# One PSUM bank for transposes, three for filter values, four buffers for decayed values in a filter stage

## The chip, the cores and the metric

The kernel runs on one core of a Trainium2 chip. TensorE (PE) multiplies matrices, VectorE (DVE), ScalarE (ACT) and GpSimd (POOL) work on tiles, SyncE (SP) issues most transfers. The metric is the device time of one execution in microseconds, the median of several runs.

## The reference

One layer of an encoder: a normalised input is projected, goes through a state-space branch (S5) and a Hyena branch, is merged, projected and normalised again. The change touches the implicit filters of the Hyena branch alone:

```python
h = jnp.sin(fr * (feats @ w1 + b1))
h = jnp.sin(fr * (h @ w2 + b2))
h = h @ w3                                           # (L, 4 * W): 2 orders, 2 directions
h = h * (jnp.exp(-t * jnp.abs(decay)) + HY_SHIFT)
h_fwd, h_bwd = h[:, :, 0], h[:, :, 1]
k = jnp.concatenate([h_fwd, jnp.zeros_like(h_fwd[:1]), jnp.flip(h_bwd[1:], axis=0)], axis=0)
k = k * lax.rsqrt(jnp.sum(k * k, axis=0, keepdims=True) + HY_EPS)
return jnp.fft.rfft(k, axis=0)
```

with L = 1024 positions and W = 1024 channels.

## The kernel before

The program is written in Python; a scheduler puts each engine's instructions into a fixed order, by the dependences, by its own model of durations and by the buffers that a pool has. An engine runs its instructions in that order and waits at each until its inputs are there and its buffer is free.

The filter stage comes first. It makes the filters in eight units of 256 channels in both directions (two orders, four quarters of the channels). Each unit has three parts.

`filter_time` goes over eight tiles of 128 positions, in the order 4, 5, 6, 7, 0, 1, 2, 3. For each, PE makes the filters' values g in one PSUM bank with two matmuls (L333, L334); ACT makes the exponential e (L336); DVE makes of both the decayed value, in the place of e (L338). ACT squares it into sq, for the first tile into acc (L342); POOL adds sq to acc (L357). The sum and the difference of the two directions (L349, L350) are made by POOL, for the first and the fourth tile (and in the first unit for the first six) by DVE. For the first four tiles they lie in so, which has one buffer, and are split in a rounded part sh (ACT, L109) and a rest sl (DVE, L113); for the last four they stay whole as ss and sd. For the fifth tile a memset of one row (L340) comes behind L338. At the end POOL folds acc (L362).

`filter_norm` sums acc over positions on PE into q (L371), which lies in the pool f_px, takes the inverse root on DVE in a chain of some twenty instructions on one or two elements per partition (L375, L119, L121, L125, L126, L381), turns a row with two transposes (L383) into the same bank and corrects ss (L386).

`filter_freq` makes the spectrum: PE multiplies sh and sl with cosines and sines (po, 96 matmuls of a unit, L404) and ss, sd (pe, 16 of two passes each, L414); ACT copies one pe to eo (L421), DVE makes ke (L425, L426) and ko (L429, L430) of it, SP stores ko. po and pe have two banks each. This part of a unit runs beside `filter_time` of the next.

Beside it `norm_in` normalises the input: its row norms go through the same chain (48 of DVE's small instructions), and then sixteen groups of four transposes (xt, L475, also in f_px) are read by ACT (xh, L479) and DVE (xl, L480). They must all be done before the projection begins (pps, L556), whose banks take the place of f_px and f_pg.

Of the kernel before, what the change touches and what calls it, by code (L numbers as in the profile page):

```python
# [9 lines left out]
F = mybir.dt.float32  # L10
# [4 lines left out]
PSUM = bass.MemoryType.PSUM  # L15
# [4 lines left out]
NCH = 256  # L20
# [80 lines left out]
class Trunk:  # L101
# [141 lines left out]
    def filters(self, ctx, top):  # L243
        tc = self.tc
        c2 = ExitStack()
        mk = lambda c, n, b, **kw: c.enter_context(tc.tile_pool(reuse_waits="tile", name=n, bufs=b, **kw))
        self.f_dve0, self.f_dve = (0, 1, 2, 3, 4, 5), (0, 3)
        sd = [None, mk(ctx, "f_sd1", 1)]
        self.f_w = mk(ctx, "f_work", 2)
        sd[0] = mk(c2, "f_sd0", 1, side="right")  # L250
        self.f_t = mk(c2, "f_time", 2, side="right")
        self.f_pk = mk(ctx, "f_pk", 1, space=PSUM)
        self.f_px, self.f_pg = (mk(c2, n, 2, space=PSUM, side="right") for n in ("f_px", "f_pg"))
        units = [(o, cq) for o in range(2) for cq in range(4)]
        sds = {}
        x = self.norm_in()
        for u in range(len(units) + 1):
            t = iter(())
            if u < len(units):
                t = self.filter_time(*units[u], sds, sd[u % 2])  # L260
            if u == 0:
                f = self.filter_freq(*units[0], sds)
                with tc.issue_after(self.f_sin.ins):
                    for i, _ in enumerate(t):
                        if i == 2:
                            self.f_next()
                        if i == 5:
                            with tc.issue_after(self.f_g.ins):
                                self.f_turn()
                        if i > 3:  # L270
                            next(f)
                f0 = 4
                continue
            if u > 1:
                f, f0 = self.filter_freq(*units[u - 1], sds), 0
            if u == len(units):
                self.filter_norm(*units[u - 1], sds)
                c2.close()
                self.weight_pools(top)
                self.proj_pools(top)  # L280
                self.prefetch()
            for i in range(12):
                next(t, None)
                if i == 0 and u < len(units):
                    with tc.high_priority(offset=40):
                        self.filter_norm(*units[u - 1], sds)
                if i >= f0:
                    with tc.issue_after(self.f_g.ins):
                        next(f)
                if i % 3 == 0:  # L290
                    with tc.issue_after(self.f_sq.ins):
                        next(x, None)
                if i == 6 and u + 1 < len(units):
                    self.filter_load(*units[u + 1])()
            for _ in t:
                pass
            next(f, None)
        for _ in x:
            pass
# [23 lines left out]
    def filter_time(self, o, cq, sds, pool):  # L323
        nc, I = self.nc, self.I
        wp = self.f_t
        fe, fo, ha, negt = self.fc
        w3h, w3l, decf = self.f_loaded.pop(0)
        sd_t = [None] * 8
        sds[o, cq] = [sd_t, None]
        for n, tt in enumerate((4, 5, 6, 7, 0, 1, 2, 3)):  # L330
            ps = self.f_pg.tile([128, 2 * NCH], F, name="g")
            tsl = slice(tt * 128, tt * 128 + 128)
            nc.tensor.matmul(out=ps, lhsT=ha[:, tsl], rhs=w3h, start=True, stop=False)  # L333
            self.f_g = nc.tensor.matmul(out=ps, lhsT=ha[:, tsl], rhs=w3l, start=False, stop=True)  # L334
            e = wp.tile([128, 2 * NCH], F, name="e", bufs=3)
            nc.scalar.activation(out=e, in_=decf, func=AF.Exp, scale=negt[:, tt:tt + 1])  # L336
            h = e
            nc.vector.scalar_tensor_tensor(out=h, in0=e, scalar=0.05, in1=ps, op0=ALU.add, op1=ALU.mult)  # L338
            if tt == 0:
                nc.vector.memset(h[0:1, NCH:2 * NCH], 0.0)  # L340
            sq = wp.tile([128, 2 * NCH], F, name="sq" if n else "acc", bufs=2 if n else 1)
            self.f_sq = nc.scalar.activation(out=sq, in_=h, func=AF.Square)  # L342
            if tt > 3:
                so = wp.tile([128, 2, NCH], F, name="so", bufs=1)
                sd = [so[:, 0], so[:, 1]]
            else:
                sd = [pool.tile([128, NCH], F, name=f"{m}{tt}") for m in ("ss", "sd")]
            eng = nc.vector if n in (self.f_dve0 if o == cq == 0 else self.f_dve) else nc.gpsimd
            eng.tensor_tensor(out=sd[0], in0=h[:, 0:NCH], in1=h[:, NCH:], op=ALU.add)  # L349
            eng.tensor_tensor(out=sd[1], in0=h[:, 0:NCH], in1=h[:, NCH:], op=ALU.subtract)  # L350
            if tt > 3:
                hl = [pool.tile([128, 2, NCH], R, name=f"{m}{tt}") for m in ("sh", "sl")]
                self.split(so, *hl, hi_eng="dve" if o == cq == 0 and n < 4 else "act")
                sd = hl
            sd_t[tt] = sd
            if n:
                nc.gpsimd.tensor_tensor(out=acc, in0=acc, in1=sq, op=ALU.add)  # L357
            else:
                acc = sq
            sds[o, cq][1] = acc  # L360
            if n == 7:
                nc.gpsimd.tensor_tensor(out=acc[:, 0:NCH], in0=acc[:, 0:NCH], in1=acc[:, NCH:], op=ALU.add)  # L362
            yield
# [1176 lines left out]
```

## Time and profile before

| | us |
|---|---|
| median of three runs | 1416.13 (1413.56 to 1418.54) |
| profiled execution | 1413.96 |
| its span | 1412.2 |

| engine | busy us | share of the span |
|---|---|---|
| PE | 1346.7 | 95% |
| PE's weight loads | 1135.9 | 80% |
| DVE | 1014.1 | 72% |
| ACT | 515.1 | 36% |
| POOL | 416.6 | 29% |

Busy is the time in which an engine has an instruction in work, including what that instruction waits for inside; idle time before an instruction is put down to what released it. Shares of the whole span are averages over stages with different limits.

### The profile page before, as it was taken

To read this page: it belongs to the slowest core of one execution; us is meant where nothing else is said; L and a number is where in the kernel's file an instruction comes from. 1 tells how busy PE (TensorE), PEld (TensorE's weight loads), DVE (VectorE), ACT (ScalarE), POOL (GpSimd) and SP (SyncE) were. 2 spreads that over 40 slices of the span, in tenths; PEclk is the share of its full clock that TensorE was granted. 3 is DMA by queue.
4 is the path that set the end of the run, shared out by engine and by line. 5 is a ranking of instruction groups with operands and counts; after the bars stand their busy time and mean duration, and the time that the engine had idled before them with its cause. 6 is when DMAs were issued, how large, how long until landed. Compare 5 with 4: busy or idle time off the path is not lost.

```text
span 1412.2 us, 19536 instructions
## 1 busy us (share of the span) xinstructions
PE 1346.7 (95%) x7219; PEld 1135.9 (80%) x7219; DVE 1014.1 (72%) x1934; ACT 515.1 (36%) x737; POOL 416.6 (29%) x343
## 2 busy tenths in 40 slices
PE   5888899999999999999999997999999999999997
PEld 3777798888888887788788885998888889878886
DVE  7999997699599887414479997663899836843632
ACT  5576664222332333333322222443222234422422
POOL 3766675000000000223112213743013223322322
PEclk9999999999999999999999998999999999999999
DMA  8222224865695554566985588769888988755431
GB/s 278 94 78 75 77 100 146 200 173 137 164 301 132 124 124 103 134 173 155 307 244 173 172 241 264 216 179 315 258 268 268 292 247 245 220 161 134 139 112 64
DMA packets 188556, 257.24 MB, mean 182 GB/s; under 512 B 23069, under 2 KB 144153, under 8 KB 185724
## 3 DMA queue, kind: packets, MB, share of 16 engines
q1 hardware_dynamic: 148492, 151.32, 34.0%
q0 software_dynamic: 12608, 43.79, 15.6%
q10 hardware_dynamic: 27360, 60.88, 12.0%
q8 instruction: 57, 0.93, 0.3%
q14 instruction: 39, 0.32, 0.1%
HBM read 147.49 MB, written 76.82 MB: 159 GB/s over the span
## 4 chain that ended last, share of the span: by engine, by line
PE 72%; DVE 18%; DMA 5%; issue 3%; ACT 1%; POOL 1%; SPq 0%; ACTq 0%; DVEq 0%; POOLq 0%
PE pps L556 43%; PE ops L1441 6%; PE iv L643 5%; PE po L404 4%; PE fwo L695 3%; DMA zc<-c_zc_lo_d 2%; PE pe L414 2%; PE pps L536 2%; DVE rsq_h L125 2%; DVE e L338 1%; PE fwe L695 1%; DMA d_y<-x 1%; DVE st L1274 1%; PE zt L680 1%; DVE st L1272 1%
## 5 line engine op out<-in xcount | busy, mean ns | idle before, releaser
L512 POOL DMA_DIRECT2D wlo<-wraw x76 | 66.3, 872 | 673.3 <-ACT wlo L511 530.2
L556 PE MATMUL pps<-xh,whi 128*128 128x512 f32 x848 | 214.2, 400 | 3.2 <-DVE cv L581 3.2
L556 PE MATMUL pps<-xl,whi 128*128 128x512 f32 x848 | 212.3, 397 | 0.0
L556 PE MATMUL pps<-xh,wlo 128*128 128x512 f32 x848 | 210.2, 396 | 0.0
L556 PEld LDWEIGHTS pps<-xh,whi 128*128 128x128 f32 x848 | 158.0, 189 | 39.5 <-ACT wlo L511 3.6
L556 PEld LDWEIGHTS pps<-xh,wlo 128*128 128x128 f32 x848 | 157.9, 188 | 36.8
L556 PEld LDWEIGHTS pps<-xl,whi 128*128 128x128 f32 x848 | 157.3, 188 | 36.3 <-issue 0.2
L510 ACT CAST whi<-wraw 128x1024 fp32r<-128x1024 f32 (+1 forms) x76 | 74.7, 982 | 285.7 <-PE pps L556 254.9
L404 PE MATMUL po<-sh,fo 128*128 128x256 f32 x512 | 101.1, 292 | 6.0 <-DVE sh L111 5.1
L643 PE MATMUL iv<-ic,y 128*128 128x256 f32 (+1 forms) x752 | 97.2, 287 | 5.5 <-POOL y L113 3.1
L643 PEld LDWEIGHTS iv<-ic,y 128*128 128x128 f32 x752 | 95.4, 194 | 8.1 <-POOL y L113 4.0
L404 PEld LDWEIGHTS po<-sh,fo 128*128 128x128 f32 x512 | 84.0, 197 | 8.3 <-DVE sh L111 6.1
L357 POOL TENSOR_TENSOR acc<-acc,sq 128x512 f32<-128x512 f32 x56 | 75.9, 1356 | 24.5 <-ACT sq L342 23.0
L511 ACT ACTIVATE wlo<-whi 128x1024 fp32r<-128x1024 f32 (+1 forms) x76 | 74.9, 985 | 20.7 <-PE pps L556 20.6
L113 DVE TENSOR_TENSOR y<-yraw,y 128x512 fp32r<-128x512 f32 x60 | 55.0, 938 | 28.2 <-ACT y L109 28.2
L404 PE MATMUL po<-sl,fo 128*128 128x256 f32 x256 | 74.2, 290 | 1.0 <-DVE sl L113 1.0
L579 DVE SCALAR_TENSOR_TENSOR cv<-pps,cw,cv 128x1023 f32<-128x1023 f32 x24 | 30.7, 1281 | 59.5 <-ACT cv L578 59.5
L109 ACT CAST y<-yraw 128x512 fp32r<-128x512 f32 x64 | 39.0, 619 | 55.9 <-DMA yraw<-d_y 27.4
L404 PEld LDWEIGHTS po<-sl,fo 128*128 128x128 f32 x256 | 50.4, 197 | 2.2 <-DVE sl L113 1.3
L578 ACT ACTIVATE cv<-pps,cb,cw 128x1024 f32<-128x1024 f32 x24 | 29.0, 1208 | 62.1 <-PE pps L556 43.9
L333 PE MATMUL g<-w3h,ha 128*128 128x512 f32 x64 | 33.3, 520 | 18.6 <-DVE e L338 17.6
L695 PE MATMUL fwo<-z,zc 128*128 128x256 f32 x384 | 49.9, 283 | 0.0
(447 smaller groups left out, 2788.7 us busy)
## 6 DMA issues: line engine op xcount, KB each, us to landing
wlo<-wraw POOLq DMA_DIRECT2D x64, 512.0 KB, 5.7
wraw<-w_in SPq DMA_DIRECT2D x56, 512.0 KB, 5.2
kspec<-ko SPq DMA_DIRECT2D x32, 512.0 KB, 3.6
kt<-kspec SPq DMA_DIRECT2D x32, 512.0 KB, 5.1
yraw<-d_y SPq DMA_DIRECT2D x64, 256.0 KB, 5.3
d_y<-x ACTq DMA_DIRECT2D x28, 512.0 KB, 5.5
d_m<-cv ACTq DMA_DIRECT2D x16, 512.0 KB, 2.6
d_z<-z ACTq DMA_DIRECT2D x8, 1024.0 KB, 5.5
```

The source lines that it names most:

```text
L109: nc.scalar.copy(out=hi, in_=src)
L113: e.tensor_tensor(out=lo, in0=src, in1=hi, op=ALU.subtract)
L333: nc.tensor.matmul(out=ps, lhsT=ha[:, tsl], rhs=w3h, start=True, stop=False)
L357: nc.gpsimd.tensor_tensor(out=acc, in0=acc, in1=sq, op=ALU.add)
L404: nc.tensor.matmul(out=po[:, part], lhsT=fo[a][:, 12 * (jj % 2) + b], rhs=sd[4 + i][d][:, part], start=n == 0 and part == 0, stop=n == 11 ...
L510: nc.scalar.copy(out=hi, in_=raw)
L511: nc.scalar.activation(out=lo, in_=hi, func=AF.Copy, scale=-1.0)
L512: nc.gpsimd.dma_start(out=lo, in_=raw, accum_op=ALU.add)
L556: self.summed = nc.tensor.matmul(out=ps[:, hf * 512:hf * 512 + 512], lhsT=w[:, kc], rhs=part(x, kc, hf), start=a == 0 and p == 0 and kc == ...
L643: self.rotated = nc.tensor.matmul(out=dst, lhsT=lhsT, rhs=self.ic[b, j][:, cols], start=first, stop=last)
L695: nc.tensor.matmul(out=out, lhsT=zc[a][:, b], rhs=z[:, :, d, zi], start=start and n == 0, stop=stop and n == 3 * len(prods) - 1)
L1441: nc.tensor.matmul(out=pss[cs.start][:, 0:cs.stop - cs.start], lhsT=m[:, kc, ts], rhs=w[kc][:, cs], start=kc == 0 and p == 0, stop=kc == 7 ...
```

## The change

The pool f_px, which holds the groups of transposes and the norms' sums q, gets one PSUM bank in place of two; f_pg, which holds g, gets three in place of two. The tile e gets four buffers in place of three.

```diff
-        self.f_px, self.f_pg = (mk(c2, n, 2, space=PSUM, side="right") for n in ("f_px", "f_pg"))
+        self.f_px, self.f_pg = (mk(c2, n, b, space=PSUM, side="right") for n, b in (("f_px", 1), ("f_pg", 3)))
...
-            e = wp.tile([128, 2 * NCH], F, name="e", bufs=3)
+            e = wp.tile([128, 2 * NCH], F, name="e", bufs=4)
```

The scheduler writes another order of the filter stage for it. DVE, in the last unit, before: from the first sl of the unit to the second.

```order
L113 TENSOR_TENSOR sl_2317<-so,sh_2316 128x512
L429 TENSOR_TENSOR ko<-ke,po 128x512
L430 TENSOR_TENSOR ko<-ke,po 128x512
L338 SCALAR_TENSOR_TENSOR e<-e,g 128x512
L375 TENSOR_SCALAR qs<-q 128x2
L119 TENSOR_SCALAR nrm<-qs 128x2
L480 SCALAR_TENSOR_TENSOR xl<-xt,par,xh 128x512
L121 TENSOR_SCALAR qs<-qs 128x2
L338 SCALAR_TENSOR_TENSOR e<-e,g 128x512
L125 SCALAR_TENSOR_TENSOR rsq_h<-nrm,qs 128x1 x2
L113 TENSOR_TENSOR sl_2378<-so,sh_2377 128x512
```

The same engine and place after, from the first sl to the third.

```order
L113 TENSOR_TENSOR sl_2317<-so,sh_2316 128x512
L429 TENSOR_TENSOR ko<-ke,po 128x512
L430 TENSOR_TENSOR ko<-ke,po 128x512
L113 TENSOR_TENSOR sl_2378<-so,sh_2377 128x512
L338 SCALAR_TENSOR_TENSOR e<-e,g 128x512
L340 MEMSET e 1x256
L480 SCALAR_TENSOR_TENSOR xl<-xt,par,xh 128x512
L113 TENSOR_TENSOR sl_2406<-so,sh_2405 128x512
```

The three sl stand close together, and the norm's chain comes behind them. POOL in the last unit, before:

```order
L362 TENSOR_TENSOR acc<-acc 128x256
L349 TENSOR_TENSOR so<-e 128x256
L350 TENSOR_TENSOR so<-e 128x256
L357 TENSOR_TENSOR acc<-acc,sq 128x512 x2
L349 TENSOR_TENSOR so<-e 128x256
L350 TENSOR_TENSOR so<-e 128x256
L357 TENSOR_TENSOR acc<-acc,sq 128x512
L349 TENSOR_TENSOR ss_2467<-e 128x256
L350 TENSOR_TENSOR sd_2468<-e 128x256
L357 TENSOR_TENSOR acc<-acc,sq 128x512
```

and POOL there after:

```order
L362 TENSOR_TENSOR acc<-acc 128x256
L349 TENSOR_TENSOR so<-e 128x256
L350 TENSOR_TENSOR so<-e 128x256
L349 TENSOR_TENSOR so<-e 128x256
L350 TENSOR_TENSOR so<-e 128x256
L349 TENSOR_TENSOR ss_2467<-e 128x256
L350 TENSOR_TENSOR sd_2468<-e 128x256
L349 TENSOR_TENSOR ss_2487<-e 128x256
L350 TENSOR_TENSOR sd_2488<-e 128x256
L357 TENSOR_TENSOR acc<-acc,sq 128x512 x2
```

The two pairs of so stand side by side, and the accumulations have moved behind ss. PE behind the last g of the stage (the last L333, L334 of before), before:

```order
L475 MATMUL xt<-ident,xr 128x128 x4
L333 MATMUL g<-w3h,ha 128x512
L334 MATMUL g<-w3l,ha 128x512
L414 MATMUL pe<-sd_2193,fe 128x256
L414 MATMUL pe<-sd_2236,fe 128x256
L414 MATMUL pe<-ss_2192,fe 128x256
L414 MATMUL pe<-ss_2235,fe 128x256
L414 MATMUL pe<-sd_2144,fe 128x256
L414 MATMUL pe<-sd_2164,fe 128x256
L414 MATMUL pe<-ss_2143,fe 128x256
L414 MATMUL pe<-ss_2163,fe 128x256
```

and PE there after:

```order
L333 MATMUL g<-w3h,ha 128x512
L334 MATMUL g<-w3l,ha 128x512
L414 MATMUL pe<-sd_2193,fe 128x256
L414 MATMUL pe<-sd_2236,fe 128x256
L414 MATMUL pe<-ss_2192,fe 128x256
L414 MATMUL pe<-ss_2235,fe 128x256
L383 MATMUL q<-ident,qs 128x128 x2
L475 MATMUL xt<-ident,xr 128x128 x4
L414 MATMUL pe<-ss_2143,fe 128x256
L414 MATMUL pe<-ss_2163,fe 128x256
L475 MATMUL xt<-ident,xr 128x128 x4
L414 MATMUL pe<-sd_2144,fe 128x256
```

A norm's transposes and, with two more further down, four groups of xt have moved behind the last g.

## Rows read from the trace of the kernel before

**Rows 1.** Two windows: PE, PEld, DVE, ACT, POOL busy (instructions), PE clock, DMA.

```profile
20.00:228.00 208.00, 181.60 (x1070) 157.99 (x1068) 201.80 (x421) 133.05 (x241) 144.20 (x145) 0.95 0.29 105
...
228.00:290.00 62.00, 61.83 (x347) 53.68 (x348) 41.67 (x241) 15.58 (x19) 10.14 (x12) 1.00 0.81 207
```

**Rows 2.** Who waited for whom from 12 to 240 us: in total, times, longest.

```profile
PEld g L333 <- DVE e L338: 23.5, 15, 4.4
...
POOL ss L349 <- DVE e L340: 6.2, 2, 3.9
```

**Rows 3.** The same of DVE alone, from 20 to 228 us.

```profile
DVE sl L113 <- ACT sh L109: 2.8, 4, 1.0
DVE e L338 <- PE g L334: 0.9, 3, 0.4
```

**Rows 4.** DVE's groups, 20 to 228 us: count | busy us, mean ns | idle before.

```profile
L113 DVE TENSOR_TENSOR sl<-so,sh 128x512 fp32r<-128x512 f32 x32 | 25.3, 790 | 2.9 <-ACT sh L109 2.8
L125 DVE SCALAR_TENSOR_TENSOR rsq_h<-nrm,qs 128x1 f32<-128x1 f32 x42 | 20.8, 529 | 0.2
...
L350 DVE TENSOR_TENSOR so<-e 128x256 f32<-128x256 f32 x18 | 15.0, 834 | 0.0
...
L386 DVE SCALAR_TENSOR_TENSOR ss<-q,ss 1x256 f32<-1x256 f32 x7 | 2.8, 396 | 0.4 <-PE q L383 0.4
```

**Rows 5.** Timeline from 161 us, POOL and DVE: start us, us, engine, instruction.

```profile
161.32 1.29 POOL L357 TENSOR_TENSOR acc<-acc,sq 128x512 f32<-128x512 f32 x1 [4.55 <-ACT sq L342]
...
162.00 0.64 DVE L119 TENSOR_SCALAR nrm<-qs 128x2 int32<-128x2 int32 x1
162.57 0.74 POOL L349 TENSOR_TENSOR so<-e 128x256 f32<-128x256 f32 x1
162.68 0.66 DVE L121 TENSOR_SCALAR qs<-qs 128x2 f32<-128x2 f32 x1
```

**Rows 6.** Timeline of DVE: lone durations at 98, 104 and 196 us.

```profile
98.38 0.16 DVE L119 TENSOR_SCALAR nrm<-qs 128x2 int32<-128x2 int32 x1
...
103.89 0.22 DVE L125 SCALAR_TENSOR_TENSOR rsq_h<-rs,ssq 128x1 f32<-128x1 f32 x1
...
196.43 0.42 DVE L350 TENSOR_TENSOR so<-e 128x256 f32<-128x256 f32 x1
```

**Rows 7.** Timelines of POOL, ACT and DVE: the way from sl to sl.

```profile
197.85 1.39 POOL L349 TENSOR_TENSOR ss<-e 128x256 f32<-128x256 f32 x1 [3.92 <-DVE e L340]
...
211.47 0.74 POOL L349 TENSOR_TENSOR so<-e 128x256 f32<-128x256 f32 x1 [1.27 <-DVE sl L113]
212.16 0.75 POOL L350 TENSOR_TENSOR so<-e 128x256 f32<-128x256 f32 x1
...
213.19 0.61 ACT L109 CAST sh<-so 128x512 fp32r<-128x512 f32 x1
...
210.71 0.68 DVE L113 TENSOR_TENSOR sl<-so,sh 128x512 fp32r<-128x512 f32 x1
211.31 0.68 DVE L429 TENSOR_TENSOR ko<-ke,po 128x512 f32<-128x512 f32 x1
...
212.50 0.68 DVE L338 SCALAR_TENSOR_TENSOR e<-e,g 128x512 f32<-128x512 f32 x1
```

**Rows 8.** Timelines of PE, ACT and DVE and the chain (its rows name no operation): the hand-over.

```profile
211.24 0.63 PE L475 MATMUL xt<-ident,xr 128*128 128x128 f32 x4
...
218.05 0.69 ACT L479 ACTIVATE xh<-xt,par 128x512 fp32r<-128x512 f32 x1 [1.80 <-PE xt L475]
...
230.89 0.74 DVE L480 SCALAR_TENSOR_TENSOR xl<-xt,par,xh 128x512 fp32r<-128x512 f32 x1
...
227.31 0.68 DVE L426 TENSOR_TENSOR ke<-pe,eo 128x512 f32<-128x512 f32 x1
...
228.13 2.40 PE pe L414 x10
...
245.56 3.26 PE pps L556 x14
```

## The prediction, made before the changed kernel ran

> **What bounds the kernel now.** I first read the windows of the profile [rows 1]. The filter stage runs until 228 us; in the stretch behind it PE is busy for 61.83 of 62.00 us, so the kernel's time hangs on when that stage ends and how much of PE's work is then still undone. Inside the stage the picture is another: from 20 to 228 us DVE is busy 201.80 of 208 us, PE only 181.60. DVE bounds the stage, with 6.2 us of idle time in all.
>
> Next I read who waited for whom [rows 2]. The longest is that of PE's weight loads for DVE's decayed value (23.5 us; PE's matmuls behind them wait for the same): a group g of filter values needs a PSUM bank, and with two banks it waits for the value before last. That is what the change gives a third bank for. But the waiting engine is not the one that bounds: DVE's own waits are short [rows 3], 2.8 us for ScalarE's cast sh, 0.9 us for g, little else. A third bank and a fourth buffer can take from DVE at most these, and of the 6.2 us only the 0.9 us is a wait for g itself.
>
> What DVE's busy time is made of matters next [rows 4]. An instruction on one element per partition (L125) takes 0.22 us alone, yet the mean of 42 is 529 ns; L350 takes 0.42 us alone and 834 ns in the mean [rows 4, 6]. The timeline shows why [rows 5]: POOL's sum ended at 162.61 and DVE's L119 at 162.64; POOL's next ended at 163.31 and L121 at 163.34. DVE instructions with SBUF inputs wait for the POOL instruction that is running, one after the other, and the profile counts it as busy. Over the lone durations (0.22, 0.42 and, for L113, 0.68 [rows 6, 7]) that is 42 x 0.31 + 18 x 0.41 + 32 x 0.11 = 24 us in three groups alone, four times DVE's idle time. The Trainium skill says the same (SBUF — State Buffer, section "SBUF: two separate sides"): the pair of ports that the two engines share is an exclusive lock, and whoever comes second "fully blocks". The rows agree to 0.03 us.
>
> **The change, part by part.** No instruction is added or removed, none has another size. What changes is memory, and through it the order that the scheduler writes. From the projection's first tile on the order is the same row for row on every engine, but for one small instruction of DVE, so no term lies there.
>
> *More buffers for e and g.* e and g run further ahead. Worth on PE: nothing, since PE then waits for DVE at the next place. Worth on DVE: between 0 and the 6.2 us of idle time; less than nothing only through the order, below.
>
> *The order of POOL and DVE in a unit.* This is where I expect the loss. The tile so has one buffer: POOL's sums for the second and third time tile wait until DVE has written sl of the tile before. Before, DVE has much to do between one sl and the next, the norm's chain of small instructions among it, and POOL two accumulations (L357). After, POOL has so, so side by side in most units, and DVE has the sl instructions close together, the norm behind them. From one sl to the next the way leads through POOL's two sums and ScalarE's cast: 211.47 to 212.91 on POOL, 0.61 us for the cast, three hand-overs of some 0.08 us (211.39 to 211.47 is one): 2.3 us [rows 7]. DVE's work in between in the last unit is one pair L429/L430 (from 211.31 to 212.50 in before [rows 7]) = 1.2 us, then e, xl and a memset of one row, 0.6 + 0.7 + some 0.2 = 1.5 us. So 1.1 and 0.8 us of idle DVE there. Counted over the order in the same way I find ten such places: units 4 to 7 two each (1.9, 1.4, 1.0 and 1.9 us), and units 1 and 2 about 3.1 and 2.2 us, 11.5 us together. Unit 3 keeps long distances. The bounds of this term are -6.2 us (all of DVE's idle time goes, none comes) and +11.5 us. A wait of this kind has a row: sl for sh, 2.8 us in 4 cases, 0.7 us each [rows 3]. I take ten at 0.7 us, less the 2.8 us that they replace: **+4.2 us**.
>
> *One bank for transposes and norms.* The 16 groups of four transposes (xt) and the norm's sums q now share one bank: each xt must wait until ScalarE's xh (0.69 us) and DVE's xl (0.74 us) have read the one before [rows 8]. Inside the stage PE has 26 us of idle time, which hides it. At the hand-over it doesn't. Before, all 64 transposes stand ahead of the last g, and PE runs without a gap from 228.13 us, released by DVE's L426 [rows 8]. After, four groups of four stand behind the last g. I walk it from the end of the last L381 ahead of that place: two transposes of the norm some 0.5 us with the hand-over, xt 0.8, xh and xl 1.6 with hand-overs (DVE at +2.9), L425 and L426 1.3 more (+4.2): only then has pe its bank and PE no more gaps. DVE has less to do ahead of that L381 than before ahead of L426: left behind are L386, two xl, two ke and without one e, 0.4 + 1.5 + 1.3 - 0.7 = 2.5 us more [rows 4, 7, 8], so it stands at 228.0 - 2.5 = 225.5 and PE runs gapless from 229.7. Two groups of transposes are then still in front of it, 2 x 0.85 = 1.7 us (0.63 by the engine's row, some 0.85 with the weight loads ahead). 229.7 + 1.7 - 228.1 = **+3.3 us**. Bounds: 0 (transposes hidden where PE waits anyway) and 4.5 us (all four groups and a full xh, xl pair exposed).
>
> *Clock.* The granted clock in the stage is 0.95 of the full 2.4 GHz, in the stretch behind it 1.00 [rows 1]; PE isn't the bound where it is lower, so I put nothing for it.
>
> *POOL itself* is busy 144.20 of 208 us [rows 1]; it has room, and more accumulations at the unit's end cost nothing by themselves. Weights for the projection: their path starts when the last e, acc and so are free, and PE has 17 us of other work until it needs them (228.13 to 245.56 [rows 8]), so a delay of 2 us is covered.
>
> Sum: 4.2 + 3.3 = +7.5 us on 1413.96 us, the profiled execution's own time (span 1412.2), is 1421.5. That execution stands 2.2 us under the median of the three runs, 1416.13; a median of runs of the changed kernel should lie nearer to 1423.6. I predict 1422.
>
> **Rivals.** *Fewer port waits, faster.* The order of DVE's small instructions against POOL's sums is new in every unit, and the 24 us of waits hang on it. For it: while DVE idles for so, POOL runs undisturbed, and the clashes of that pair are spared; the 48 small instructions of the row norms, in unit 3, stand in blocks of up to six, no longer with ke, so and ko between them. If a third goes (8 us) and half of DVE's idle time with it (3 us), the hand-over's 3.3 us are outweighed: 1413.96 - 8 - 3 + 3.3 = 1406. Against it: POOL's work is the same, over two thirds of the stage, whoever meets it.
>
> *It does nothing that counts.* The buffers take 3 us of DVE's idle time, the hand-over gives them back, the sl distances are filled by port waits that would come anyway: 1414 by the profiled execution, 1416 by the median.
>
> *Port waits rise, much slower.* Before, the memset L340 stands behind the norm's chain, and POOL waits for it (6.2 us in two cases [rows 2], 3.92 us in one of them [rows 7]): half of the chain runs while POOL stands still. After, the memset stands ahead of the chain in units 4 to 7, so POOL has ss, ss and two accumulations ready, some six more instructions without a pause, each of which can hold back one of the chain's. 4 units x 6 x 0.5 us (0.64 and 0.66 for L119 and L121 instead of 0.16 [rows 5, 6]) = 12 us on top of the 7.5: 1433. It decides from the point at which POOL is not idle in the chain any more. By the rule of the Trainium skill quoted above (SBUF — State Buffer) each of these instructions would hold one back whenever it starts first, and the time would be this 1433 us.
>
> **How the numbers follow.** About 0.3%, 4.2 us on 1416.13, is what a measurement of this kernel can tell from no change. The forecast (slower by 3 to 12 us) has 0.45, fewer port waits 0.20, no effect 0.22, more port waits 0.13. Alone, the forecast's own range is 1417 to 1428. For 8 in 10 I reach into both neighbours: low 1409, high 1434. Faster by over 0.3%: 0.18, nearly all of the first rival. Within: 0.36, the second rival and the lower part of the forecast (0.12 or so). Slower: 0.46, the rest of it and the third.
>
> **What would show it.** Right: PE's wait for e (L338) is much shorter and yet DVE stays the fullest engine; DVE has more waits of sl for sh, the longest near 2 us; PE's last gap of the stage ends at some 234 us. Wrong: DVE's idle time from 20 us to the hand-over falls below 6 us; the means of L125 and L350 move by more than 100 ns either way, which decides between the first and the third rival; the gapless stretch begins before 228 us; or PE's busy time behind the stage differs.

## The result and the profile after

The changed kernel takes 1451.78 us (median of 4 runs, 1450.21 to 1453.50), the kernel before beside it 1417.34: a ratio of 1.0249, with a 95% interval of 1.0233 to 1.0266. It is slower, as forecast, by 34.4 us and not by 6 to 8; the time lies 18 us above the range. The profiled execution took 1453.5 us (span 1451.7), 39.5 us more than that of the kernel before; the rows below compare these two executions.

The windows show where. First the two windows of [rows 1] in the kernel after (window and its length, then PE, PEld, DVE, ACT and POOL busy with instructions, PE's clock, DMA share, GB/s):

```profile
20.00:228.00 208.00, 163.46 (x899) 136.85 (x899) 181.79 (x372) 118.10 (x213) 127.44 (x128) 0.85 0.26 95
228.00:290.00 62.00, 54.49 (x329) 48.03 (x328) 43.75 (x104) 24.20 (x38) 24.93 (x27) 0.92 0.41 118
```

In the 208 us in which DVE was busy for 201.80 before, it is now busy for 181.79, and 372 of its instructions are done where 421 were. Fixed windows hold different work, so I took the stretch from 20 us to the projection's first tile pps as well, once for the kernel before and once for the kernel after:

```profile
20.00:245.20 225.20, 198.67 (x1196) 174.48 (x1195) 212.92 (x456) 138.95 (x248) 151.79 (x153) 0.95 0.32 114
```

```profile
20.00:283.60 263.60, 211.55 (x1201) 179.69 (x1200) 219.84 (x456) 141.72 (x249) 152.38 (x154) 0.86 0.27 98
```

The same 456 instructions of DVE and the same 1200 or so of PE take 38.4 us longer, nearly all of the 39.5 us between the two executions. Of the 38.4, DVE is 6.9 us busier and 31.5 us idler (43.8 in place of 12.3). Looked at from PE it is 12.9 us busier and 25.5 idler. DVE was the full engine of this stage; it is still the fullest, but now none is full.

The waits from 12 to 270 us of the kernel after (engine and line, whom it waited for, us in total, times, longest) answer to [rows 2, 3]:

```profile
PEld g L333 <- DVE e L338: 42.1, 24, 4.8
POOL so L349 <- DVE sl L113: 37.1, 11, 12.5
...
PEld q L383 <- DVE qs L381: 18.2, 9, 5.4
...
ACT acc L342 <- PE q L371: 10.7, 5, 4.0
...
DVE sl L113 <- ACT sh L109: 9.2, 11, 2.2
DVE xl L480 <- ACT xh L479: 8.6, 4, 3.9
...
DVE ke L425 <- PE pe L414: 7.3, 5, 2.8
```

PE's wait for e, which a third bank was to shorten, has grown from 23.5 to 42.1 us. PE's weight loads for the norm's turned row (L383) stand 18.2 us for the end of DVE's chain, before 3.1. DVE itself waits in many places, a few us each: xl is new to its list, and ke's wait for pe, 7.3 us, was 0.4 us before. DVE's groups from 20 to 260 us, after [rows 4] (count, busy us, mean ns, idle time before and its releaser):

```profile
L113 DVE TENSOR_TENSOR sl<-so,sh 128x512 fp32r<-128x512 f32 x32 | 27.0, 843 | 9.3 <-ACT sh L109 9.2
L125 DVE SCALAR_TENSOR_TENSOR rsq_h<-nrm,qs 128x1 f32<-128x1 f32 x42 | 23.9, 605 | 0.2
...
L350 DVE TENSOR_TENSOR so<-e 128x256 f32<-128x256 f32 x18 | 13.8, 769 | 0.0
...
L480 DVE SCALAR_TENSOR_TENSOR xl<-xt,par,xh 128x512 fp32r<-128x512 f32 x13 | 9.6, 736 | 4.7 <-ACT xh L479 4.7
L425 DVE TENSOR_TENSOR ke<-pe,eo 128x512 f32<-128x512 f32 x13 | 8.9, 686 | 6.9 <-PE pe L414 6.4 <-ACT eo L421 0.5
```

The means of the instructions that meet POOL have moved by under 80 ns (L113 from 790, L125 from 529, L350 from 834): the port waits are much as they were (3.6 us more busy time in the three groups together).

Last the hand-over, PE's timeline of the kernel after (start us, us, engine, instruction, idle time before and releaser), the answer to [rows 8]:

```profile
254.83 0.32 PE L383 MATMUL q<-ident,qs 128*128 128x128 f32 x1 [4.97 <-DVE qs L381]
...
260.83 1.62 PE L414 MATMUL pe<-sd,fe 128*128 128x256 f32 x3 [0.50 <-DVE ke L426]
...
283.57 1.75 PE L556 MATMUL pps<-xh,whi 128*128 128x512 f32 x6
```

PE runs nearly without gaps from 260.83 us, before from 228.13: 32.7 us of the loss are there by then. From there to pps it is 22.7 us, before 17.1 (228.13 to 245.21), 5.6 us more. Not all of that is work left behind: PE has 16 more instructions in this stretch, two groups of xt and eight matmuls of pe, an estimated 2.5 us. Until 265.7 us the granted clock is 0.52, and the first twelve pe matmuls take 4.95 us; at a granted clock of 1.00 four take 0.87 us (209.31 to 210.18), so twelve would take an estimated 2.6, and the clock costs 2.3 us. Another 0.6 us is a wait for L386.

### The profile page after: what moved, and what is told of

Read it like the earlier page. It is cut to its first block, busy times and chain, and to the rows that moved or that the text cites. A ratio compares the mean times of both kernels' runs of the same rounds, so it can differ in the third digit from the quotient of the medians.

```text
span 1451.7 us, 19514 instructions
## 1 busy us (share of the span) xinstructions
PE 1360.9 (94%) x7219; PEld 1143.3 (79%) x7219; DVE 1022.1 (70%) x1934; ACT 517.2 (36%) x737; POOL 408.6 (28%) x343
## 4 chain that ended last, share of the span: by engine, by line
PE 75%; DVE 16%; DMA 4%; issue 2%; POOL 1%; ACT 1%; SPq 0%; DVEq 0%; ACTq 0%; POOLq 0%
PE pps L556 44%; PE ops L1441 6%; PE iv L643 6%; PE fwo L695 3%; PE po L404 3%; PE pe L414 3%; DMA zc<-c_zc_lo_d 2%; DVE rsq_h L125 2%; PE pps L536 2%; PE fwe L695 2%; DVE sl L113 1%; DVE e L338 1%; PE zt L680 1%; DVE st L1274 1%; DVE st L1272 1%
## 5 line engine op out<-in xcount | busy, mean ns | idle before, releaser
L643 PEld LDWEIGHTS iv<-ic,y 128*128 128x128 f32 x752 | 98.6, 201 | 4.1 <-DVE y L113 2.1
L113 DVE TENSOR_TENSOR y<-yraw,y 128x512 fp32r<-128x512 f32 x60 | 54.5, 929 | 30.0 <-ACT y L109 29.7
L333 PE MATMUL g<-w3h,ha 128*128 128x512 f32 x64 | 35.6, 557 | 33.3 <-DVE e L338 32.4
```

The lines of the kernel that those rows point to most:

```text
L113: e.tensor_tensor(out=lo, in0=src, in1=hi, op=ALU.subtract)
L643: self.rotated = nc.tensor.matmul(out=dst, lhsT=lhsT, rhs=self.ic[b, j][:, cols], start=first, stop=last)
```

## The experiments

### Each part of the change alone

The change has three numbers: banks of f_px, banks of f_pg, buffers of e (before 2, 2, 3; after 1, 3, 4). Four kernels set them apart; theory A was the shared single bank, B the order of g, C the fourth buffer.

```diff
 self.f_px, self.f_pg = (mk(c2, n, b, ...) for n, b in (("f_px", 1), ("f_pg", 2)))   # e bufs=3: c_px1
 self.f_px, self.f_pg = (mk(c2, n, b, ...) for n, b in (("f_px", 1), ("f_pg", 3)))   # e bufs=3: a_banks
 self.f_px, self.f_pg = (mk(c2, n, b, ...) for n, b in (("f_px", 2), ("f_pg", 2)))   # e bufs=4: b_e4
 self.f_px, self.f_pg = (mk(c2, n, b, ...) for n, b in (("f_px", 1), ("f_pg", 2)))   # e bufs=4: d_px1e4
```

The single bank alone (c_px1): 

> One bank for xt and q in place of two, nothing else changed (f_px 1, f_pg 2, e three buffers; one PSUM bank lies idle). Theory A, the shared bank: PE stands in its fixed order at xt and at the norm's transposes, DVE starves behind it; this carries most of the 34 us, 1432 to 1450 us, PE's waits at xt and q for L381, L480 some 20 us longer than before. Theory B, the order of g: running g further ahead pushes the sums and the norm together, the bank matters only at the hand-over; 1414 to 1421 us. Theory C, the fourth buffer of e: 1414 to 1421 us as well.

Both edits of the banks (a_banks): 

> Both edits of the banks (f_px 1, f_pg 3), e with three buffers as before. Theory A: like the changed kernel or a few us better, 1440 to 1455 us. Theory B: the third bank of g alone lets g run ahead, 1435 to 1455 us, with the same loss of DVE's time in units 2 and 4. Theory C: e holds g back as before, 1414 to 1425 us.

The fourth buffer alone (b_e4): 

> The fourth buffer of e alone (f_px 2, f_pg 2). Theory A: nothing, 1412 to 1421 us, since xt and q keep two banks. Theory B: g has two banks and cannot run further ahead on PE, 1412 to 1424 us. Theory C: most of the loss is here, 1435 to 1455 us.

The single bank with the fourth buffer (d_px1e4): 

> One bank for xt and q together with the fourth buffer of e, g with two banks as before (one bank idle). Theory A: 1432 to 1450 us, like the single bank alone. Theory B: no third bank for g, so 1414 to 1424 us. Theory C: 1435 to 1455 us, like the fourth buffer alone.

Each ratio here and below is to the kernel before as it was measured beside that kernel (1415 to 1418 us).

| f_px, f_pg, e | us | ratio to before (95%) |
|---|---|---|
| 1, 2, 3 | 1443.0 | 1.0165 (1.0134 to 1.0197) |
| 1, 3, 3 | 1444.6 | 1.0188 (1.0165 to 1.0211) |
| 2, 2, 4 | 1425.2 | 1.0047 (1.0026 to 1.0068) |
| 1, 2, 4 | 1443.5 | 1.0175 (1.0156 to 1.0195) |
| 1, 3, 4 (after) | 1451.8 | 1.0249 (1.0233 to 1.0266) |

Taking one bank from xt and q costs some 25 of the 34 us by itself. Theory A has the times of all three kernels with the single bank; B and C fall by c_px1, which they put at 1414 to 1421 us. A's mechanism does not hold as it stands: in c_px1 PE's waits at q and xt for L381 and L480 were to grow by some 20 us and grew from 2.3 to 8.2. Beside the single bank a third bank for g changes nothing clear of noise, nor does the fourth buffer; only both together add more, some 9 us by the medians (their ratios are 1.0188 and 1.0175, that of both 1.0249). And the fourth buffer alone, which adds no work, costs 7 us: a miss of all three theories; A had it at nothing.

### Is it the sharing, or the single bank of the transposes?

My first theory of how the bank costs (A1): the norm keeps it from its sums (L371) to its corrected row (L386), 10 to 16 us, and the transposes wait behind. The rival (A2): a group of transposes needs PE, ACT and DVE in turn, and one bank makes each group wait for all three. k_split gives q a bank of its own, so that each user has one; l_short and m_short_af let the norm claim the bank (take it for a tile of its own) twice, for the sums and for the turned row.

```diff
+        self.f_pq = mk(c2, "f_pq", 1, space=PSUM, side="right")                        # k_split
-        q = self.f_px.tile([128, 512], F, name="q", tag="xt")
+        q = self.f_pq.tile([128, 512], F, name="q")
```

```diff
-        r = q[:, NCH:]                                       # l_short (1, 2, 3), m_short_af (1, 3, 4)
+        r = self.f_px.tile([128, 512], F, name="r", tag="xt")[:, NCH:]
```

The split (k_split): 

> One bank for xt and one bank of its own for q (f_px 1, new pool for q 1, f_pg 2, e three buffers: the same eight banks as before, only no longer shared). Theory A1, the norm holds the bank: q keeps it for 10 to 16 us of each unit (from L371 to L386), and the transposes then come in a burst; with a bank of its own for q the loss goes, 1414 to 1424 us, DVE's idle time per unit back under 2 us. Theory A2, the round trip of a transposes' group (xt, xh, xl) through one bank is itself the loss: 1432 to 1445 us, like one bank for both (1443).

Short holds on the single bank (l_short): 

> One bank for xt and q (f_px 1, f_pg 2, e three buffers), but the norm takes it twice for a short time, once for the sums (to L375) and once for the turned row (L383 to L386), and not through its chain of DVE's small instructions. Theory A1: most of the 25 us goes, 1416 to 1428 us. Theory A2: 1435 to 1445 us, as with the long hold.

Short holds in the changed kernel (m_short_af): 

> The changed kernel (f_px 1, f_pg 3, e four buffers) with the same short holds of the norm. Theory A1: the 25 us of the bank go and what the fourth buffer costs (7 us) stays, 1420 to 1436 us. Theory A2: 1445 to 1453 us.

k_split: 1417.09 us, 1.0016 (1.0006 to 1.0025). All but some 2 us of the loss is gone with one bank for the transposes, so A2 falls: it is not the transposes' own round trip but that the two users take turns. l_short: 1442.5 us, 1.0193 (1.0172 to 1.0214), and m_short_af: 1451.3 us, 1.0246 (1.0224 to 1.0269): nothing gained, where A1 expected most of the loss back. PE's timeline of l_short shows that this edit did not do what it was meant to do:

```profile
140.39 0.58 PE L371 MATMUL q<-ones,acc 128*128 128x1 f32 x4
...
150.30 0.40 PE L383 MATMUL r<-ident,qs 128*128 128x128 f32 x2 [2.14 <-DVE qs L381]
...
151.21 0.66 PE L475 MATMUL xt<-ident,xr 128*128 128x128 f32 x4 [0.50 <-DVE ss L386]
```

DVE read the sums at 141.36 us, and the bank then stood empty until r at 150.30. In the program r is the next claim after q, and the bank goes round in the order of the claims; xt, ready or not, comes behind r.

### Claims in another order

p_late and p_late_af write r and its correction after the unit's fourth step, so that two groups of xt come between q and r. The other three give so a second buffer: g_so2af in the changed kernel, f_so2 in the kernel before, p_late_af_so2 in p_late_af.

```diff
                     with tc.high_priority(offset=40):
-                        self.filter_norm(*units[u - 1], sds)
+                        turn = self.filter_norm(*units[u - 1], sds)     # ends ahead of the transposes L383
+                if i == 4 and u < len(units):
+                    with tc.high_priority(offset=40):
+                        turn()                                          # claims r, L383, L386
```

```diff
-                so = wp.tile([128, 2, NCH], F, name="so", bufs=1)
+                so = wp.tile([128, 2, NCH], F, name="so", bufs=2)
```

The late second hold (p_late): 

> One bank for xt and q (f_px 1, f_pg 2, e three buffers), the norm in two short holds as before, but its second one (L383, L386) written after the fourth step of the unit, so that two groups of xt come between the two in the order in which the tiles claim the bank. Theory A1 (the bank goes round in the order of the claims, and the norm's 10 to 16 us lie in it): 1416 to 1428 us, xt groups between the sums and the turned row in the trace. Theory A3 (a single bank costs by its round trips, however the claims are ordered): 1435 to 1447 us.

The same in the changed kernel (p_late_af): 

> The changed kernel (f_px 1, f_pg 3, e four buffers) with the same late second hold of the norm. Theory A1: 1422 to 1436 us, what is left above before is that of the buffers of g and e. Theory A3: 1443 to 1453 us.

Two buffers of so in the changed kernel (g_so2af): 

> The changed kernel with two buffers for so. The prediction's step on the order of POOL and DVE (so waits for sl of the tile before) said some 4 us: 1444 to 1450 us if it is that, POOL's wait for sl (37 us) gone. Theory A: POOL's waits are a symptom, 1447 to 1455 us. If the so chain is what starves DVE in units 2 and 4: 1425 to 1440 us.

Two buffers of so in the kernel before (f_so2): 

> The kernel before with two buffers for so. If so is no bound of its own there (DVE is busy 201.8 of 208 us): 1412 to 1421 us. If POOL's waits for sl (18 us before) hold DVE up: 1402 to 1411 us.

Late hold and two buffers of so (p_late_af_so2): 

> The changed kernel with the late second hold and two buffers for so, both suspected causes taken away. If they are the whole loss and add up (25 and 9 us): 1414 to 1422 us. If g's third bank and e's fourth buffer are then worth something: under 1412 us. If a third cause is left: 1424 to 1440 us.

p_late: 1435.4 us, 1.0130 (1.0103 to 1.0158), a quarter of the loss back and no more (its interval and that of c_px1 overlap); the trace does have the groups between (q at 196.77, xt at 202.23 and 206.95, r at 212.93). p_late_af: 1455.5 us, 1.0271 (1.0243 to 1.0298), nothing back. Both stand outside A1's ranges: A1 was not the main thing.

g_so2af: 1443.1 us, 1.0210 (1.0182 to 1.0238), by the ratios 5 and by the medians 9 us better than the changed kernel (the intervals just overlap; the time lies between the ranges given), while DVE's wait of sl for sh falls from 9.2 to 2.5 us. By the medians that is all that the changed kernel stands above its single bank, by the ratios about half. POOL's wait for sl, which was to be gone, is still 23.1 of 37.1 us. And it is no rule: the same edit makes the kernel before slower (f_so2: 1424.5 us, 1.0056, 1.0036 to 1.0076) and gives p_late_af nothing (p_late_af_so2: 1458.2 us, 1.0286, 1.0259 to 1.0313); both lie above every range that I had given.

### The two halves of the shared bank

So I gave one half of the norm a bank of its own at a time, all else as in c_px1: in s_qx xt and the sums q share and r is alone, in s_rx xt and r share and q is alone. A3 was now that any taking of turns costs.

```diff
+        self.f_pq = mk(c2, "f_pq", 1, space=PSUM, side="right")
-        r = q[:, NCH:]
+        r = self.f_pq.tile([128, 512], F, name="r")[:, NCH:]              # s_qx; in s_rx q is the one in f_pq
```

xt with q (s_qx): 

> e three buffers, f_pg 2, f_px 1 for xt and the norm's sums q, and a bank of its own for the norm's turned row r (L383 to L386). Claims on the shared bank: q, released at L375 after some 1 to 4 us, then xt, xt, xt. Theory A1 (what costs is that transposes stand behind the norm's chain of 10 to 16 us): 1414 to 1426 us. Theory A3 (every claim that takes turns with the other user costs): 1428 to 1440 us.

xt with r (s_rx): 

> The other half: f_px 1 for xt and the norm's turned row r, a bank of its own for the sums q. Claims on the shared bank in the order written: r, xt, xt, xt; r comes only when the norm's chain is done, and xt behind it. Theory A1: nearly the whole loss of the single bank, 1432 to 1445 us. Theory A3: about half, 1424 to 1434 us.

s_qx: 1433.5 us, 1.0099 (1.0068 to 1.0131), 16 us above before. s_rx: 1426.5 us, 1.0051 (1.0028 to 1.0073), 9 us. Both lie in A3's ranges and outside A1's. Together that is about the 25 us of c_px1, and A1 had it the wrong way round: transposes behind the norm's chain (s_rx) cost the lesser part, though the two intervals just touch, and its 9 us are little more than the 7 and 8 us that b_e4 and f_so2 lose, where no bank is shared more than before. In the larger one (s_qx) it is the sums that are late. In the kernel before, acc is folded by POOL (L362) and summed on PE 0.7 us later:

```profile
209.39 0.81 POOL L362 TENSOR_TENSOR acc<-acc 128x256 f32<-128x256 f32 x1
```

```profile
210.87 0.50 PE L371 MATMUL q<-ones,acc 128*128 128x1 f32 x4
```

The same unit in the kernel after, POOL, DVE and PE: acc is ready at 205.08, but the last transposes of the unit hold the bank until xl has ended at 211.20, and q, where PE's fixed order has it, comes at 213.54:

```profile
204.34 0.74 POOL L362 TENSOR_TENSOR acc<-acc 128x256 f32<-128x256 f32 x1
```

```profile
210.45 0.75 DVE L480 SCALAR_TENSOR_TENSOR xl<-xt,par,xh 128x512 fp32r<-128x512 f32 x1
```

```profile
213.54 0.50 PE L371 MATMUL q<-ones,acc 128*128 128x1 f32 x4
```

Over the last five units, from the end of L362 to the start of L371, it is 4.9, 1.5, 0.8, 0.7 and 2.1 us before; 12.7, 8.7, 7.8, 8.9 and 9.9 in c_px1; 10.7, 9.8, 8.6, 6.3 and 6.2 in s_qx; 19.4, 12.1, 8.5, 12.6 and 12.4 after.

Summed over these units the wait goes with the loss, if not strictly: 10 us before, 12 in k_split, 42 in s_qx, 48 in c_px1, 49 in l_short, 65 after. So the third bank and the fourth buffer, on top of the single bank, come with a still later q. That is a parallel and not a proof, and it is not the whole loss: b_e4 and s_rx stand 7 and 9 us above before with 13 and 14 us of this wait.

### Sums that don't stand behind transposes

Theory A4: q is the urgent claim, since the norm hangs on it and acc, with one buffer, stays taken until then; with one bank it stands behind the unit's last xt, which nobody hurries. w_early3 is s_qx with the same groups written in the unit's first four steps; w_acc2 is s_qx with a second buffer for acc.

```diff
-                if i % 3 == 0:
+                if i in (0, 1, 2, 3):                                    # w_early3
                     with tc.issue_after(self.f_sq.ins):
                         next(x, None)
```

```diff
-            sq = wp.tile([128, 2 * NCH], F, name="sq" if n else "acc", bufs=2 if n else 1)
+            sq = wp.tile([128, 2 * NCH], F, name="sq" if n else "acc", bufs=2)   # w_acc2
```

Transposes early (w_early3): 

> As s_qx (xt and the sums q share one bank, r has its own; 1433 us), but the groups of transposes are written in the unit's first four steps in place of every third step, so that the next unit's q does not stand behind a late group. Theory A4 (the norm's sums come 6 to 11 us after acc is folded, since the bank is still with the unit's last transposes; before it was 1 to 5 us): 1416 to 1426 us, q within 1 to 5 us of the folded acc. Theory A3 (two users on one bank cost, whatever the order of claims): 1430 to 1440 us.

Two buffers of acc (w_acc2): 

> As s_qx (1433 us), with two buffers for acc in place of one. acc is kept until q has summed it, and the next unit's first square needs its place. If q's lateness costs by this: 1416 to 1426 us, with q as late as in s_qx. If it costs by the norm's late end (ss, pe): 1430 to 1437 us.

w_early3: 1420.5 us, 1.0033 (1.0018 to 1.0047), in A4's range and under A3's. Two thirds (by the ratios) to over three quarters (by the medians) of this loss are gone with the bank still shared; the intervals leave room down to some 30%. q comes 2.5, 0.8, 0.5, 0.1 and 5.5 us after the folded acc. The programs of s_qx and w_early3 have a line more, so L363 and L372 are L362 and L371 of the kernel before. s_qx, POOL, then PE:

```profile
192.18 0.74 POOL L363 TENSOR_TENSOR acc<-acc 128x256 f32<-128x256 f32 x1
```

```profile
201.56 0.50 PE L372 MATMUL q<-ones,acc 128*128 128x1 f32 x4
```

w_early3, POOL, then PE, which now waits for acc itself and for nothing else:

```profile
209.34 0.80 POOL L363 TENSOR_TENSOR acc<-acc 128x256 f32<-128x256 f32 x1
```

```profile
210.20 0.61 PE L372 MATMUL q<-ones,acc 128*128 128x1 f32 x4 [0.31 <-POOL acc L363]
```

w_acc2: 1424.9 us, 1.0056 (1.0040 to 1.0071): about half of the 16 us back. In two of the five units q is still late (12.5 and 6.3 us; 1.2, 3.6 and 4.4 in the others), so the new order moved q too, and the half is not acc's alone by this run. The stretch from 20 us to pps of s_qx and then of w_early3 (profiled executions of 1434.4 and 1417.4 us; the second is the fastest of its ten):

```profile
20.00:264.50 244.50, 207.15 (x1195) 177.10 (x1195) 215.68 (x455) 140.85 (x249) 149.99 (x154) 0.94 0.30 105
```

```profile
20.00:248.60 228.60, 199.94 (x1205) 175.58 (x1203) 211.58 (x456) 140.54 (x249) 155.50 (x154) 0.96 0.32 114
```

DVE's idle time falls from 28.8 to 17.0 us, near the 12.3 of the kernel before.

### g and e without a shared bank

With one bank for pe in place of two there is room for a third bank of g beside xt and q with a bank each.

```diff
 f_px 1, f_pq 1, f_pg 2, e bufs=3, pe bufs=1        # u0_pe1
 f_px 1, f_pq 1, f_pg 3, e bufs=4, pe bufs=1        # u_pe1
```

The base (u0_pe1): 

> Base for the next: xt and q with a bank each (1417 us so far), and pe with one bank in place of two, which leaves a bank free. 1420 to 1445 us, by how much PE waits for pe to be read.

With the third bank and the fourth buffer (u_pe1): 

> The same with the free bank given to g (three) and with four buffers of e: the two other edits of the change, with no shared bank. If they cost something through the order of POOL and DVE, as on top of the shared bank (9 us): 5 to 12 us above the base. If they only hurt together with the shared bank: within 4 us of the base. If they gain what DVE's idle time gives: 2 to 6 us below it.

u0_pe1: 1444.5 us, 1.0171 (1.0133 to 1.0209); u_pe1: 1448.4 us, 1.0201 (1.0163 to 1.0239). The two intervals overlap, so this pair says only that the two buffers gain nothing here either; whether they cost 4 us is not settled. The base is itself 27 us slower than the kernel before, by its single bank for pe, which may hide a gain or a loss.

## Why the prediction was wrong, point by point

- **DVE bounds the stage.** Right of the kernel before, and the reason why I looked no further: the sum held that nothing but DVE's own work and its two known waits could move the end. In the kernel after DVE is busy for 219.84 of 263.60 us (83%, before 95%), and the end is set by turns between engines.
- **One bank for transposes and norms: the step that failed.** I priced the shared bank at the hand-over alone and wrote that inside the stage "PE has 26 us of idle time, which hides it". Idle time hides work of PE; what the bank made late was not PE's work but a claim, the norm's sums, and with it a buffer (acc, for whose place ACT waited 10.7 us, before 4.7) and a chain on DVE; how these two share the loss is not settled. The bound of the term inside the stage stood at zero with no row for it. The single bank cost 25 us alone; 32.7 us of the loss were there when PE's last gap ended. The forecast way, slower, came true, but through a term that I had put at nothing: that part is luck.
- **The hand-over.** Forecast +3.3 us, with 4.5 as the upper bound. PE's gapless stretch began 32.7 us later, nearly all of it brought along from the stage. The stretch behind it grew by 5.6 us. The two groups of transposes that I had counted there are there, with eight pe matmuls that I had not; the clock's 2.3 us I had not either. From the first turned row to the gapless stretch it was 6.0 us (254.83 to 260.83) where my walk had 4.2 from the end of L381.
- **The order of POOL and DVE.** The mechanism was there and about the size: forecast ten waits of sl for sh, 7.0 us in total, the longest near 2 us; measured 11 waits, 9.2 us, the longest 2.2. g_so2af took 6.7 us of them and 5 to 9 us of the time away. But a_banks has 7.6 us of these waits and is no slower than c_px1 with 3.4, so I do not call the two equal.
- **More buffers for e and g.** Put between nothing and a gain of 6.2 us. The fourth buffer of e alone costs 7 us, a second buffer of so in the kernel before 8 us. In both the order is new; what in it costs was not tried.
- **Clock, put at nothing.** The granted clock from 20 us to pps fell from 0.95 to 0.86, and the same matmuls kept PE busy for 12.9 us more. At the hand-over, where PE runs without gaps, an estimated 2.3 us of it lie on the path. Since DVE's ke waits for pe now, more may; how much was not measured.
- **Port waits.** Neither rival on them came true: DVE's busy time rose by 6.9 us for the same 456 instructions, where one rival had 12 more and the other 8 fewer. A clash in the kernel after looks as in [rows 5], POOL's L350 from 214.37 to 215.12 and DVE's L121 until 215.15:

```profile
214.37 0.75 POOL L350 TENSOR_TENSOR sd<-e 128x256 f32<-128x256 f32 x1
```

```profile
214.48 0.67 DVE L121 TENSOR_SCALAR qs<-qs 128x2 f32<-128x2 f32 x1
```

  The Trainium skill's lock (SBUF — State Buffer, section "SBUF: two separate sides") is in these rows again, to 0.03 us. That each of some 24 instructions would be held back, as the third rival had it, the 6.9 us do not bear out.
- **What would show it.** PE's wait for e should have been much shorter and was longer (42.1 us), and the last gap was to end at 234 us and ended at 260.83. DVE stayed the fullest engine (219.84 us, PE 211.55), and the sign of sl and sh came true. None of the four signs of being wrong appeared: DVE's idle time rose, L125 and L350 moved by under 80 ns, the gapless stretch began later, and PE behind the stage was busy for 1139 us in both kernels. No sign that I had named watched the bank.
- **The range.** It reached to 1434 us by a rival on another mechanism. With the bank's term left open upwards inside the stage, it would have had to hold the time that one bank costs when it is the longest chain of claims; in the trace of the kernel before, q held its bank for 12 to 16 us in each of units 4 to 7, and three or four groups of xt held theirs for 2 to 10 us each, in units of some 26 us: in a single bank these follow one another, and that alone fills it.

What is shown: the loss of the single bank (25 us) comes from two users taking turns in it (c_px1 against k_split), and of its larger half (16 us) some two thirds go when the transposes are claimed earlier, and with them the late sums. That the sums' lateness, and nothing else in the new order, is what cost them is argued and not shown. What is open: the other half (9 us), the 9 us that the third bank and the fourth buffer add together, the 7 us of the fourth buffer alone, and most of the clock's part. No kernel here is faster than the one before; k_split, with a bank each, is nearest (1.0016).

## What to carry to other kernels

Before two users are put into one buffer, write down the order in which they claim it, and ask of each claim who stands ahead of it and who hangs on it: an urgent, short claim behind an unhurried one is as late as that one, and idle time of the engine that makes the claim hides nothing of it. If a buffer must be shared, write the unhurried user's claims so that none of them is last before the urgent one. Where a scheduler writes the order, more buffers are not free either: in the kernel before, a buffer more for e or for so cost half a per cent.

## What the hardware showed that I had not expected

PE's granted clock hung together with its waits more closely than I had reckoned with. In the kernel after, four transposes took 0.60 us where PE had run without a pause, and 1.11 us behind the wait of 4.97 us for L381; the pe matmuls beside them 1.03 and 1.91 us. The granted clock is 1.00 from 205 to 211 us and 0.50 from 256.5 to 260.8, the two levels of 2.4 and 1.2 GHz:

```profile
208.88 0.60 PE L475 MATMUL xt<-ident,xr 128*128 128x128 f32 x4
...
210.18 1.03 PE L414 MATMUL pe<-ss,fe 128*128 128x256 f32 x4
```

```profile
256.53 1.11 PE L475 MATMUL xt<-ident,xr 128*128 128x128 f32 x4 [0.50 <-DVE ss L386]
257.44 1.91 PE L414 MATMUL pe<-ss,fe 128*128 128x256 f32 x4
```

So a long wait of PE can be paid for twice, in the gap and in the slower work behind it, and what waits for that work, ke here, passes it on. Not every wait is: in l_short, shown above, four transposes behind a wait of 2.14 us took 0.66 us. The Trainium skill says that the clock has these two levels and that the chip sets them by how busy PE has been of late (TensorE: Matmul & The Clock Gate, section "Part 1: The HAM clock gate"); the rows agree.
